# Two-layer hybrid encoder on one core: the start's transfers reordered, the final norm's last columns taken from PSUM, the output stored in three parts

## The chip, the cores and the metric

The kernel runs on 1 core of a Trainium2 chip. The metric is the device time of one execution in microseconds (us). Engines are named as in the profile: PE is TensorE, ACT ScalarE, DVE VectorE, POOL GpSimd, SP SyncE, which here only issues transfers.

## The reference, cut to what matters

256 tokens of 1024 channels pass through two layers. Each has a token mixer and a gated MLP, both behind an RMSNorm and with a residual, and a last RMSNorm makes the output. All is float32.

```python
def _rmsnorm(x, g):
    y = x * lax.rsqrt(jnp.mean(x * x, axis=-1, keepdims=True) + EPS)
    return y * g

h = x
for layer in range(DEPTH):                      # DEPTH = 2
    h = h + _token_mixer(_rmsnorm(h, norm1[layer]), w_in[layer], ...)
    h = h + _conv_ffn(_rmsnorm(h, norm2[layer]), w_up[layer], ..., w_down[layer])
return _rmsnorm(h, norm_f)
```

## The kernel before, in words

Tokens lie on the 128 partitions in two tiles, t = 0 and 1; `h` (128 x 2 x 1024) holds the residual stream in SBUF for the whole program. Each weight is streamed once from HBM by SP, in pieces named `raw`, and split into a rounded high part `wh` (ACT, L191 or L199) and a low part `wl` (DVE, L192 or L200). Products are float32r matmuls: high x high, low x high, high x low. The scheduler of the framework orders each engine's instructions; in the first stage (`values_of_x`, L702) the order is that of the code.

**The start.** `begin` (L337) issues the first transfers: pieces of the value weights `raw` (L142), pieces of x into `h` (L343), and the 8 x 128 row `grows` of norm1 (L349). PE meanwhile multiplies a tile of ones by itself (`warm`, L374, result unused), transposes the row so that the gains lie on partitions (L369; DVE copies it to `gcol`, L370), and transposes the first 256 columns of x for both tiles (`turn_x`, L715). One more warming matmul follows (`wait`, called at L790). ACT scales the first weights by `gcol` (L199) as it rounds them, so the first product (`product`, L762) needs the row, the first piece of x and the first piece of weights. The norm's factor of each token is applied to the finished sums.

**The end.** `residual_mm` (L567) adds `w_down`'s product to the residual: all but the last 4 of 22 chunks are added for both tiles and all columns into four PSUM banks `ps[t][c]` of 512 columns; the last 4 chunks (`held`) are then added one segment of columns after another (L593): for t = 0 two of 512, for t = 1 columns 0 to 511, 512 to 767 and 768 to 1023. The third segment of t = 1 shares its bank with the second; so DVE first adds the bank's partial sum to `h` (L599), and the last 4 chunks go to a tile of their own, `res2_ps` (L600; profile and order call it `res_ps`). After each segment `Norm.add` (L456) lets DVE add the sum to `h` (L460), ACT square the new columns and sum them up (L462, which in the profile is an ACTIVATE and the read of its accumulator), DVE multiply them by the final gain into `xn` (L467), and POOL add up the sums (L469, L471). After a tile's last segment POOL takes the power -1/2 (L474), and `store` (L509) scales `xn` by this factor `rstd`, columns 0 to 511 on DVE and the others on ACT, and sends both halves out on SP. The store of t = 0 is run within t = 1's segments.

## Time and profile before

| | us |
|---|---|
| median of 3 runs (860.9, 860.95, 861.31) | 860.95 |
| profiled execution, whole | 860.72 |
| its span, first to last instruction | 858.9 |
| PE busy | 850.1 |

A row of the timeline gives the start in us from the span's start, the duration, the engine, the line, the operation and its tiles, and in brackets the engine's idle time before it with what ended it. `SPq` and `ACTq` are the engines' queues issuing a transfer. PE's matmuls overlap, so the distance of two starts, not the duration, is what one of a row of them costs. A row of the chain gives start, duration and what the end of the program hung on at that time.

### The profile page before, as it was taken

Reading aid. Unit: us, or ns where it says so; the run is one execution under the profiler, and the core shown is the slowest. Engines: PE = TensorE matmul, PEld = TensorE weight load, DVE = VectorE, ACT = ScalarE, POOL = GpSimd, SP = SyncE. Lnnn points to the kernel's source line nnn. Section 1 sums busy time; section 2 is a strip of 40 time slices with the busy share of each in tenths; the row PEclk is TensorE's granted clock in tenths of the full one; section 3 lists DMA queues with packets and bytes.
Section 4 is the critical chain, followed back from the end, with each engine's and each line's share of the span. In section 5 each row is a group of like instructions: output and inputs, shape, how many; then the busy total and the mean of one; then the engine's idle time right before and its main releaser. Section 6 shows DMA issues by size and latency. Waiting matters only on the chain.

```text
span 858.9 us, 11272 instructions
## 1 busy us (share of the span) xinstructions
PE 850.1 (99%) x4036; PEld 714.3 (83%) x4036; DVE 646.1 (75%) x910; ACT 478.7 (56%) x702; POOL 19.0 (2%) x54
## 2 busy tenths in 40 slices
PE   8999999999999999999999999999999999999997
PEld 7888898888888888888888889888888888888885
DVE  4967989566757699999555598886567757998974
ACT  7735475444535576767344446654445436666762
POOL 1120000000010000000000000000000000000001
PEclk9999999999999999999999999999999999999999
DMA  9687585763846777877526776648558376777751
GB/s 316 201 280 248 173 286 157 221 234 123 295 171 212 238 241 242 249 238 270 196 98 201 231 235 206 223 156 247 199 201 285 103 214 211 242 242 240 240 197 50
DMA packets 99628, 185.02 MB, mean 215 GB/s; under 512 B 9630, under 2 KB 26734, under 8 KB 99572
## 3 DMA queue, kind: packets, MB, share of 16 engines
q1 hardware_dynamic: 98900, 182.83, 65.0%
q0 software_dynamic: 528, 1.34, 0.6%
q8 instruction: 32, 0.52, 0.2%
q14 instruction: 24, 0.20, 0.1%
q10 hardware_dynamic: 144, 0.13, 0.0%
HBM read 160.12 MB, written 1.07 MB: 188 GB/s over the span
## 4 chain that ended last, share of the span: by engine, by line
PE 99%; DMA 0%; ACT 0%; issue 0%; POOLq 0%; DVE 0%; POOL 0%; ACTq 0%
PE rows_ps L649 61%; PE res_ps L563 6%; PE res_ps L564 6%; PE res_ps L565 6%; PE v_ps L649 5%; PE proj_ps L535 3%; PE v_ps L765 3%; PE proj_ps L537 2%; PE s_ps L1053 1%; PE o_ps L1128 1%; PE s_ps L1048 1%; PE o_ps L1124 1%; PE xt_ps L496 1%; PE pool_ps L528 0%; PE pool_ps L527 0%; PE pool_ps L529 0%
## 5 line engine op out<-in xcount | busy, mean ns | idle before, releaser
L192 DVE TENSOR_TENSOR wl<-raw,wh 128x1024 fp32r<-128x1024 f32 x278 | 337.0, 1218 | 148.0 <-ACT wh L191 145.6
L649 PE MATMUL rows_ps<-wh,x 128*128 128x512 f32 x1344 | 420.1, 391 | 0.0
L191 ACT CAST wh<-raw 128x1024 fp32r<-128x1024 f32 x278 | 288.9, 1048 | 212.2 <-PE rows_ps L649 129.8
L649 PEld LDWEIGHTS rows_ps<-wh,x 128*128 128x128 f32 x1344 | 252.4, 188 | 52.1
L649 PE MATMUL rows_ps<-wl,x 128*128 128x512 f32 x672 | 261.7, 389 | 0.0
L649 PEld LDWEIGHTS rows_ps<-wl,x 128*128 128x128 f32 x672 | 126.3, 188 | 25.6
L563 PE MATMUL res_ps<-wh,actq 128*128 128x512 f32 (+1 forms) x152 | 57.5, 379 | 0.0
L565 PE MATMUL res_ps<-wh,actk 128*128 128x512 f32 (+1 forms) x152 | 57.5, 378 | 0.0
L564 PE MATMUL res_ps<-wl,actq 128*128 128x512 f32 (+1 forms) x152 | 57.5, 378 | 0.0
L649 PE MATMUL rows_ps<-wh,po 128*128 128x512 f32 x128 | 41.2, 393 | 0.0
L563 PEld LDWEIGHTS res_ps<-wh,actq 128*128 128x128 f32 x152 | 28.6, 188 | 5.4
L565 PEld LDWEIGHTS res_ps<-wh,actk 128*128 128x128 f32 x152 | 28.6, 188 | 5.3
L564 PEld LDWEIGHTS res_ps<-wl,actq 128*128 128x128 f32 x152 | 28.6, 188 | 5.3
L535 PE MATMUL proj_ps<-x,wh 128*128 128x512 f32 x128 | 32.2, 394 | 0.0
L684 DVE STREAM_TRANSPOSE up_rows<-rows_ps 128x512 f32<-128x512 f32 x40 | 26.3, 693 | 3.1 <-PE rows_ps L649 3.1
L649 PEld LDWEIGHTS rows_ps<-wh,po 128*128 128x128 f32 x128 | 24.1, 188 | 4.9
L462 ACT ACTIVATE junk<-h 128x512 f32<-128x512 f32 (+1 forms) x20 | 10.9, 547 | 30.8 <-DVE h L460 30.8
L1356 ACT ACTIVATE yg<-a,prm 128x256 f32<-128x256 f32 x44 | 26.5, 602 | 1.5
L563 PE MATMUL res_ps<-wh,m 128*128 128x512 f32 (+1 forms) x72 | 26.9, 374 | 0.0
L535 PEld LDWEIGHTS proj_ps<-x,wh 128*128 128x128 f32 x128 | 23.1, 189 | 4.2
L565 PE MATMUL res_ps<-wh,m 128*128 128x512 f32 (+1 forms) x72 | 26.4, 367 | 0.0
L564 PE MATMUL res_ps<-wl,m 128*128 128x512 f32 (+1 forms) x72 | 26.4, 366 | 0.0
(214 smaller groups left out, 1051.0 us busy)
## 6 DMA issues: line engine op xcount, KB each, us to landing
raw<-in_w_in_dram SPq DMA_DIRECT2D x56, 1024.0 KB, 5.3
raw<-in_w_up_dram SPq DMA_DIRECT2D x40, 1024.0 KB, 6.3
raw<-in_w_down_dram SPq DMA_DIRECT2D x22, 1024.0 KB, 5.1
up_turned<-up_rows SPq DMA_DIRECT2D x160, 64.0 KB, 3.9
raw<-in_w_a_dram SPq DMA_DIRECT2D x8, 1024.0 KB, 5.4
raw<-in_w_o_dram SPq DMA_DIRECT2D x8, 1024.0 KB, 6.9
qk<-qk_rows SPq DMA_DIRECT2D x64, 64.0 KB, 2.1
pt<-rows SPq DMA_DIRECT2D x64, 64.0 KB, 3.7
```

Source lines behind the costliest of these rows:

```text
L191: lambda: nc.scalar.copy(out=h, in_=src),
L192: lambda: nc.vector.tensor_sub(out=l, in0=src, in1=h.bitcast(F32)),
L462: nc.scalar.activation(junk[:, 0 : cc.stop - cc.start], h[:, t, cc], AF.Square, scale=D**-0.5, accum_out=ss[:, n : n + 1],)
L535: nc.tensor.matmul(ps, wh(k), x2[:, k], start=(k == 0), stop=False)
L537: nc.tensor.matmul(ps[:, 1], wl(k), x2[:, k, 0], start=False, stop=(k == nk - 1))
L563: nc.tensor.matmul(ps, ah, wh, start=first, stop=False)
L564: nc.tensor.matmul(ps, ah, wl, start=False, stop=False)
L565: nc.tensor.matmul(ps, al, wh, start=False, stop=last)
L649: nc.tensor.matmul(ps, x2[:, 2 * n + j, part, t, :], w[:, j, :], start=(n + m == 0), stop=(n == of - 1 and m == 5),)
L684: nc.vector.transpose(out=out[:, :, t].rearrange("p j c r -> p c j r"), in_=ps[t].rearrange("p (c j r) -> p c j r", c=4, j=4),)
L765: return nc.tensor.matmul(ps[g][t], a[:, k, t, :], w[:, k % 2, :], start=k == 0 and kind == "hh", stop=k == KD - 1 and kind == "hl",)
L1356: nc.scalar.activation(y, aj, AF.Identity, bias=b, scale=w1)
```

## The change

At the start, norm1's row goes out on ACT's queue instead of POOL's, as the first transfer there; all pieces of x and of the weights go out on SP, x's first piece ahead of the weights. The transposes of t = 1 come after the warming matmul instead of ahead of it.

At the end, for the last layer only (`seeded`), t = 1's segments are done in the order 512 to 767, 0 to 511, 768 to 1023. After the first of them DVE adds the partial sum of columns 768 to 1023 to `h` as before, and then this part of `h` is split into a high and a low part (`seed`, on ACT and DVE). In the last segment PE adds both to `res2_ps`, with an identity `one_r` as the other operand, behind the first two of the four chunks; so `res2_ps` ends as the new `h` itself (`whole`), and DVE's addition at the end is left out: ACT squares and DVE multiplies straight from PSUM. `store` sends columns 0 to 319 and 320 to 639 from DVE by SP and columns 640 to 1023 from ACT by ACT's own queue.

```diff
@@ -339,14 +339,14 @@
 
         loads = [W.load_by(n) for n in (4, 4, 2, 2)]
 
-        def part_of_x(t, c, queue=nc.sync):
-            queue.dma_start(out=h[:, t, c], in_=xv[:, t, c])
+        def part_of_x(t, c):
+            nc.sync.dma_start(out=h[:, t, c], in_=xv[:, t, c])
 
         first, second, others = slice(0, 256), slice(256, 512), slice(512, D)
+        rows8 = sm.tile([KD, P], F32, tag="gain", bufs=1, name="grows")
+        nc.scalar.dma_start(out=rows8, in_=norm1[0].rearrange("(k p) -> k p", p=P))
+        part_of_x(0, first)
         next(loads[0])
-        part_of_x(0, first, nc.scalar)
-        rows8 = sm.tile([KD, P], F32, tag="gain", bufs=1, name="grows")
-        nc.gpsimd.dma_start(out=rows8, in_=norm1[0].rearrange("(k p) -> k p", p=P))
         part_of_x(1, first)
         next(loads[1])
         next(loads[0])
@@ -453,18 +453,16 @@
             self.xn = big.tile([P, 2, D], F32, tag="xn", name="xn")
             self.ss = [sm.tile([P, 4], F32, tag="ss", name="ss") for _ in range(2)]
 
-        def add(self, t, n, cc, ps=None):
+        def add(self, t, n, cc, ps, whole=False):
 
             ss = self.ss[t]
-            if ps is not None:
+            junk = sm.tile([P, 512], F32, tag="s", name="junk")[:, 0 : cc.stop - cc.start]
+            if not whole:
                 nc.vector.tensor_add(out=h[:, t, cc], in0=ps, in1=h[:, t, cc])
-            junk = sm.tile([P, 512], F32, tag="s", name="junk")
-            nc.scalar.activation(
-                junk[:, 0 : cc.stop - cc.start], h[:, t, cc], AF.Square, scale=D**-0.5,
-                accum_out=ss[:, n : n + 1],
-            )
+            new = ps if whole else h[:, t, cc]
+            nc.scalar.activation(junk, new, AF.Square, scale=D**-0.5, accum_out=ss[:, n : n + 1])
             if self.ahead is not None:
-                nc.vector.tensor_mul(out=self.xn[:, t, cc], in0=h[:, t, cc], in1=self.ahead[:, cc])
+                nc.vector.tensor_mul(out=self.xn[:, t, cc], in0=new, in1=self.ahead[:, cc])
             if n == 0:
                 nc.gpsimd.tensor_scalar_add(ss[:, 3:4], ss[:, 0:1], EPS)
             else:
@@ -508,10 +506,12 @@
 
     def store(t, r, xn):
         ov = out[0].rearrange("(m t) d -> m t d", t=2)
-        nc.vector.tensor_scalar_mul(xn[:, 0:512], xn[:, 0:512], r[:, 0:1])
-        nc.sync.dma_start(out=ov[:, t, 0:512], in_=xn[:, 0:512])
-        nc.scalar.mul(out=xn[:, 512:], in_=xn[:, 512:], mul=r[:, 0:1])
-        nc.sync.dma_start(out=ov[:, t, 512:], in_=xn[:, 512:])
+        b = slice(640, D)
+        for c in (slice(0, 320), slice(320, 640)):
+            nc.vector.tensor_scalar_mul(xn[:, c], xn[:, c], r[:, 0:1])
+            nc.sync.dma_start(out=ov[:, t, c], in_=xn[:, c])
+        nc.scalar.mul(out=xn[:, b], in_=xn[:, b], mul=r[:, 0:1])
+        nc.scalar.dma_start(out=ov[:, t, b], in_=xn[:, b])
         yield
 
     later = []
@@ -564,7 +564,7 @@
         nc.tensor.matmul(ps, ah, wl, start=False, stop=False)
         nc.tensor.matmul(ps, al, wh, start=False, stop=last)
 
-    def residual_mm(parts, n, done, hold=4, fill=None, ahead=0):
+    def residual_mm(parts, n, done, hold=4, fill=None, ahead=0, seeded=False):
 
 
 
@@ -590,16 +590,27 @@
                 held.append((i, part))
             yield
         then, half = None, None
+        seed = None
+        if seeded:
+            one_r = sm.tile([P, P], F32R, tag="u", name="one_r")
+            nc.scalar.copy(out=one_r, in_=ident)
         for t in range(2):
-            for m, cc in enumerate(SEGMENTS[t]):
+            segments = SEGMENTS[t]
+            if t and seeded:
+                segments = segments[1], segments[0], segments[2]
+            for m, cc in enumerate(segments):
                 c, c0 = divmod(cc.start, 512)
                 res = ps[t][c][:, c0 : c0 + cc.stop - cc.start]
                 if c0:
 
-                    nc.vector.tensor_add(out=h[:, t, cc], in0=res, in1=h[:, t, cc])
+                    if not seed:
+                        nc.vector.tensor_add(out=h[:, t, cc], in0=res, in1=h[:, t, cc])
                     res = mmp.tile([P, cc.stop - cc.start], F32, tag="mm", name="res2_ps")
                 for j, (i, part) in enumerate(held):
                     one(part, res, t, cc, c0 != 0 and j == 0, j == hold - 1)
+                    if c0 and j == 1:
+                        for more in seed or ():
+                            nc.tensor.matmul(res, one_r, more, start=False, stop=False)
                 if half:
                     run(half)
                     half = None
@@ -607,7 +618,13 @@
                     half = then()
                     next(half)
                     then = None
-                then = done(t, m, cc, res) or then
+                then = done(t, m, cc, res, c0 != 0 and seeded) or then
+                if t and seeded and m == 0:
+                    rest = slice(768, D)
+                    hi, lo = seed = [sm.tile([P, 256], F32R, tag="us", name="seed") for _ in range(2)]
+                    nc.vector.tensor_add(out=h[:, t, rest], in0=ps[t][1][:, 256:], in1=h[:, t, rest])
+                    nc.scalar.copy(out=hi, in_=h[:, t, rest])
+                    nc.vector.tensor_sub(out=lo, in0=h[:, t, rest], in1=hi.bitcast(F32))
         if half:
             run(half)
         rest = fill() if fill else None
@@ -786,8 +803,9 @@
             return lambda: nc.vector.tensor_sub(out=ol, in0=f, in1=oh.bitcast(F32))
 
         fs = [big.tile([P, 4, 2, P], F32, tag=tag, name="xu") for tag in ("q0", "k0")]
-        (keep0, copy0), (keep1, copy1) = turn_x(0, 0, 2), turn_x(1, 0, 2)
+        keep0, copy0 = turn_x(0, 0, 2)
         wait()
+        keep1, copy1 = turn_x(1, 0, 2)
         rest = keep0(nc.vector.tensor_copy)
         low = split(0, 0)
         rest()
@@ -1408,7 +1426,7 @@
 
         down = residual_mm(
             lambda k: acts[k], NF, lambda *a: late["norm"].add(*a),
-            fill=begin_values if l + 1 < DEPTH else None, ahead=3,
+            fill=begin_values if l + 1 < DEPTH else None, ahead=3, seeded=l + 1 == DEPTH,
         )
         count, twos, open_two = 0, [], []
```

What it moves on the engines' queues, at three places. First SP at the program's start (`raw` with a number is a piece of weights, `h` a piece of x), before:

```order
L142 DMA raw_88<-in_w_in_dram 128x512
L343 DMA h<-in_x_dram 128x256
L142 DMA raw_94<-in_w_in_dram 128x512
L142 DMA raw_88<-in_w_in_dram 128x512
L343 DMA h<-in_x_dram 128x256 x2
```

and now:

```order
L343 DMA h<-in_x_dram 128x256
L142 DMA raw_91<-in_w_in_dram 128x512
L343 DMA h<-in_x_dram 128x256
L142 DMA raw_94<-in_w_in_dram 128x512
L142 DMA raw_91<-in_w_in_dram 128x512
```

One transfer of x, which was on ACT's queue, heads SP's; every later transfer of SP stands one place further back.

Second, PE up to the first product (`gain_ps` is the transposed row, `xt_ps` the transposed x, `v_ps` the product; in brackets the semaphores waited for, DMAHW being transfers of SP and ACT, DMASW those of POOL), before:

```order
L377 MATMUL gain_ps<-ones 128x128 x4
L369 MATMUL gain_ps<-ident,grows 128x8 [waits DMASW0_49,Pool_49]
L719 MATMUL xt_ps<-ident,h 128x128 [waits DMAHW0_49]
L719 MATMUL xt_ps<-ident,h 128x128 [waits DMAHW2_49]
L377 MATMUL warm_ps<-ones 128x128
L765 MATMUL v_ps<-m_151,xuh 128x512 [waits DVE_49,Activation_49]
```

and now:

```order
L377 MATMUL gain_ps<-ones 128x128 x4
L369 MATMUL gain_ps<-ident,grows 128x8 [waits DMAHW0_49,Pool_49]
L736 MATMUL xt_ps<-ident,h 128x128 [waits DMAHW1_49]
L377 MATMUL warm_ps<-ones 128x128
L736 MATMUL xt_ps<-ident,h 128x128 [waits DMAHW3_49]
L782 MATMUL v_ps<-m_151,xuh 128x512 [waits DVE_49,Activation_49]
```

The warming matmul has moved ahead of the transposes that wait for x's second piece (each of these rows of `xt_ps` is followed by one more without a wait, left out here).

Third, ACT's last instructions, from the last split of weights on (`junk` is the square's unused result, `ss` its sum), before:

```order
L191 CAST wh_7379<-raw_7325 128x1024
L462 ACTIVATE junk,ss<-h 128x512 x2
L513 ACTIVATE xn<-xn,rstd 128x512
L462 ACTIVATE junk,ss<-h 128x512
L462 ACTIVATE junk,ss<-h 128x256 x2
```

and now:

```order
L191 CAST wh_7379<-raw_7325 128x1024
L463 ACTIVATE junk,ss<-h 128x512 x2
L513 ACTIVATE xn<-xn,rstd 128x384
L463 ACTIVATE junk,ss<-h 128x256
L626 CAST seed<-h 128x256
L514 DMA out_dram<-xn 128x384
L463 ACTIVATE junk,ss<-h 128x512
L463 ACTIVATE junk,ss<-res_ps 128x256
```

The seed's cast and the issue of t = 0's store stand between the squares, and the last square reads `res_ps` in PSUM; in both, t = 1's scaling by `rstd` follows. On DVE, t = 0's store now stands ahead of the seed's low part, this ahead of the addition of columns 0 to 511, and the last multiplication by the gain waits for ACT.

## The prediction

> **What bounds the kernel now.** I read the page first, for the share of each engine and for the chain that ended last.
>
> ```profile
> PE 850.1 (99%) x4036; PEld 714.3 (83%) x4036; DVE 646.1 (75%) x910; ACT 478.7 (56%) x702; POOL 19.0 (2%) x54
> PEclk9999999999999999999999999999999999999999
> PE 99%; DMA 0%; ACT 0%; issue 0%; POOLq 0%; DVE 0%; POOL 0%; ACTq 0%
> ```
>
> TensorE works 850.1 of 858.9 us and is 99% of the chain. The 8.8 us in which it is idle can only lie at the ends, so an edit is worth what it does to the first matmuls, to what follows the last one, and to TensorE's own work. The second view is the chain of the first 26 us.
>
> ```profile
> 1.27 3.60 DMA grows<-in_norm_dram
> ...
> 5.25 1.04 PE xt_ps L719 x4
> 6.30 0.43 PE warm_ps L377 x2
> 6.72 4.53 PE v_ps L765 x12
> ```
>
> The first 5 us belong to one 4 KB transfer, norm1's row, issued by POOL at 1.27 and landed 3.60 us later. Behind it stand four transposes (1.04), the warming matmul (0.43), and then the products of the values without a gap. The third view is the timeline of TensorE there.
>
> ```profile
> 1.04 2.50 PE L377 MATMUL gain_ps<-ones 128*128 128x128 f32 x10 [1.04 <-DVE mhalf L366]
> 5.01 0.24 PE L369 MATMUL gain_ps<-ident,grows 8*128 8x8 f32 x1 [1.46 <-DMA grows<-in_norm_dram]
> 6.48 0.76 PE L765 MATMUL v_ps<-m,xuh 128*128 128x512 f32 x1
> 9.60 0.63 PE L765 MATMUL v_ps<-wh,xul 128*128 128x512 f32 x1
> 10.03 0.53 PE L765 MATMUL v_ps<-wl,xuh 128*128 128x512 f32 x1
> 10.40 0.39 PE L765 MATMUL v_ps<-wh,xuh 128*128 128x512 f32 x1
> 10.63 0.39 PE L765 MATMUL v_ps<-wh,xul 128*128 128x512 f32 x1
> ```
>
> Two things are to be seen. TensorE warms from 1.04 to 3.54, waits 1.46 us for the row, and starts the first product at 6.48. And equal matmuls follow each other by 0.43 us (9.60 to 10.03) until about 10.3 and by 0.23 us (10.40 to 10.63) from then on. The page's row of the granted clock reads 9 in all slices and doesn't show this step; the starts do. TensorE runs at 0.23/0.43 = 0.53 of its speed until 10.3. The burst of 2.50 us did not end the slow stretch; it ended 5.3 us after work was taken up at 5.01.
>
> **The start.** The transfers are reordered, and one of two pairs of transposes now stands behind the warming matmul. These are the rows that price it.
>
> ```profile
> 0.72 0.41 ACTq L343 DMA_DIRECT2D h<-in_x_dram  x1
> 0.73 0.39 SPq L142 DMA_DIRECT2D raw<-in_w_in_dram  x1
> 1.17 0.42 SPq L343 DMA_DIRECT2D h<-in_x_dram  x1
> 1.64 0.91 SPq L142 DMA_DIRECT2D raw<-in_w_in_dram  x2
> ...
> raw<-in_w_in_dram SPq DMA_DIRECT2D x6, 256.0 KB, 3.7
> ...
> 5.49 0.72 ACT L199 ACTIVATE m<-raw,gcol 128x512 fp32r<-128x512 f32 x1 [2.84 <-DVE gcol L370]
> 6.33 0.37 ACT L726 CAST xuh<-xt_ps 128x256 fp32r<-128x256 f32 x1
> ...
> 11.51 0.37 ACT L726 CAST xuh<-xt_ps 128x256 fp32r<-128x256 f32 x1 [1.09 <-PE xt_ps L719]
> ```
>
> *The row.* It takes the ACT slot at 0.72. This trace has no small transfer on that queue at the start: at the short end the output's 2.0 us (row below), at the long end the weights' 3.7 us. So it lands between 2.7 and 4.4; I take 3.3, nearer the short end because it is 4 KB. TensorE is busy warming until 3.54 anyway, so the transposed row comes at 3.75, and t=0's two transposes (half of 1.04 for four) and the warming matmul (0.43) run until 4.7.
>
> *What is late next.* The first weights move from SP's slot at 0.73 to the one at 1.17; with 3.7 us they land at 4.87. ScalarE's high part takes 0.72, so it is done at 5.65. The second piece of x moves from 1.17 to 1.64; it lands by 5.36 at the worst, by 4.6 if its half size halves the time beyond the first 2 us; I take 4.9, and its two transposes end at about 5.4. The first product needs both and starts at about 5.6 (5.3 to 6.0 between the ends), instead of at 6.48. TensorE's pauses between 3.54 and 5.6 are then some 0.6 us instead of 1.46.
>
> *What that is worth.* The 0.88 us are won in the slow stretch. If the speed still rises at 10.3, TensorE has done 0.88 x 0.53 = 0.47 us of full-speed work more by then, and the start gives **0.47 us** (0.25 to 0.65 for the two ends). Later loads shift by one slot of 0.45 us; ScalarE, which splits them, waits for TensorE 1.09 us at 11.51, so this is covered. POOL loses the issue and makes the identity earlier, which nobody waits for.
>
> [...]
>
> **The end.** The timeline from t=1's first matmul on:
>
> ```profile
> 846.87 0.39 PE L563 MATMUL res_ps<-wh,actq 128*128 128x512 f32 x1
> 849.59 0.72 ACT L513 ACTIVATE xn<-xn,rstd 128x512 f32<-128x512 f32 x1 [1.02 <-POOL rstd L474]
> 851.84 0.42 ACT L462 ACTIVATE junk<-h 128x256 f32<-128x256 f32 x1 [0.34 <-DVE h L460]
> 852.22 0.28 PE L564 MATMUL res_ps<-wl,actq 128*128 128x256 f32 x1
> 852.34 0.28 PE L565 MATMUL res_ps<-wh,actk 128*128 128x256 f32 x1
> 852.66 0.42 DVE L460 TENSOR_TENSOR h<-res_ps,h 128x256 f32<-128x256 f32 x1 [0.25 <-PE res_ps L565]
> 853.17 0.42 ACT L462 ACTIVATE junk<-h 128x256 f32<-128x256 f32 x1 [0.83 <-DVE h L460]
> 853.50 0.19 ACT L462 ACTIVATION_READ_ACCUMULATOR junk<-h 128x1 f32 x1
> 853.83 0.19 POOL L471 TENSOR_TENSOR ss<-ss 128x1 f32<-128x1 f32 x1 [1.14 <-ACT junk L462]
> 854.10 0.57 POOL L474 TENSOR_TENSOR rstd<-ss,mhalf 128x1 f32<-128x1 f32 x1
> 854.70 0.72 ACT L513 ACTIVATE xn<-xn,rstd 128x512 f32<-128x512 f32 x1 [1.01 <-POOL rstd L474]
> 854.70 0.49 DVE L511 TENSOR_SCALAR xn<-xn,rstd 128x512 f32<-128x512 f32 x1 [1.16 <-POOL rstd L474]
> 855.21 0.33 SPq L512 DMA_DIRECT2D out_dram<-xn  x1
> 855.60 0.42 SPq L514 DMA_DIRECT2D out_dram<-xn  x1
> ...
> out_dram<-xn SPq DMA_DIRECT2D x4, 256.0 KB, 2.0
> ```
>
> *Removed:* VectorE's addition at 852.66 from the chain. TensorE ends at 852.62, the square begins at 853.17: 0.55 us. ScalarE now waits for TensorE itself; VectorE's own wait took 0.04 us, so the square begins 0.05 us after TensorE. That saves 0.50. Reading 256 columns from PSUM took ScalarE 0.37 (the cast at 6.33) against 0.42 for the square: no loss.
>
> *Added on TensorE:* two seed matmuls of 256 columns, 0.12 us each by the two starts at 852.22 and 852.34: 0.24. Net 0.26 from TensorE's end to the norm's factor.
>
> *The seed's own path.* TensorE asks for it after t=1's 12 matmuls of 256 columns, 12 of 512 and 6 more of 256: 846.87 + 12 x 0.12 + 12 x 0.23 + 6 x 0.12 = 851.8. On ScalarE its cast stands behind t=0's store, which waits for its factor until 849.59: 384 columns by share of 0.72, some 0.6; then a square (0.42 and its read, 0.5 together) and the cast, 0.4: 851.1. VectorE's low part adds 0.45: 851.55. It is in time by 0.2 us; each 0.1 us beyond that is 0.1 at the end. Behind it on VectorE stands the addition of columns 0 to 511, which would have been ready at 851.2 and now starts at 851.55; its square then ends just before the last one may start at 852.9. This is the tightest cover of the edit. The cast of the identity stands on ScalarE near 830, where
>
> ```profile
> 836.23 1.05 ACT L191 CAST wh<-raw 128x1024 fp32r<-128x1024 f32 x1 [1.66 <-PE res_ps L565]
> ```
>
> shows ScalarE waiting 1.66 us for TensorE: nothing.
>
> *Store.* VectorE's first piece falls from 512 to 320 columns: between 0.31 (by share of 0.49) and 0.49; I take 0.36. So the first issue goes out 0.26 + 0.13 earlier than 855.21. ScalarE's piece of 384 columns ends some 0.6 after the factor and is issued on its own queue; the last issue then starts near 855.2 instead of 855.60. The bytes are the same and each transfer took 2.0 us; three transfers instead of two could cost up to 0.3 us again. I take **0.35 us** for the end (0 to 0.5).
>
> VectorE's multiplication of the PSUM columns by the gain waits for ScalarE's square, as the order shows, and behind it stands the store's first piece. It begins when the square's value is read, at 853.45, and takes 0.42, while POOL needs its 0.19, 0.57 and the gaps until 854.4: covered by 0.5 us. [...]
>
> **Sum.** The profiled execution took 860.72 us, 1.8 more than its span; the median of the runs is 860.95, 0.23 above it. 860.72 - 0.47 - 0.35 = 859.9; against the median 860.1.
>
> **The rivals.**
>
> *The speed rises earlier.* For it: the pause of 1.46 us becomes some 0.6 in pieces, so the burst at 1.04 and the rest may count as one. If work from 1.04 on is counted as that from 5.01 was, the rise comes 5.3 us after it, at 6.4. Before, the slow products from 6.48 to 10.33 were worth 3.85 x 0.53 = 2.04 us of full speed; now 5.6 to 6.4 is worth 0.42, and the remaining 1.62 is done at 8.0: 2.3 us won instead of 0.47. ScalarE then has to keep up; its slack of 1.09 us at 11.51 may cost some 0.3. With the end this gives 860.95 - 2.0 - 0.35 = 858.6, or 858.2 without a loss. Against it: a burst of 2.50 us was not enough, pauses remain, and transposes fill part of the time.
>
> *The row isn't the only thing that was late.* If the weights, one slot later, or the second piece of x land at 5.5 or later, the first product stays near 6.48 and only the end is left: 860.6. For it: in the trace the transfers crowd between 1 and 5 us. Against it: 3.7 us from 1.17 is 4.87.
>
> *Slower.* A pause in the slow stretch starts the count anew. After 5.6 the first place where this could happen is the third chunk of weights: if TensorE pauses for it near 8.5, the rise comes 5.3 us after it, near 13.8. Each us by which the rise slips past 10.3 costs 0.47; it decides from a slip of 0.82/0.47 = 1.7 us. At 13.8 it costs 1.6: 861.8. Against it: at 0.43 us each, the twelve products before that place keep TensorE until 10.7, and ScalarE has the chunk split by 8.2 in the trace.
>
> **How the numbers follow.** The forecast has a chance of 0.52, the earlier rise 0.36, a start without gain 0.08, the later rise 0.04. About 0.2% (1.7 us) is what a measurement of this kernel can tell from no change. The forecast, 859.7 to 860.7 on its own, is within that, as are the start without gain and the later rise; the earlier rise is faster. With a fast edge of the forecast and a late seed on top of a later rise I give 0.40 faster, 0.57 same, 0.03 slower. The range is 858.1 to 860.9: it takes in the earlier rise and the start without gain.
>
> **What would show it.** In the changed profile: the first product's start (5.6 forecast; 6.4 or later refutes the start), the place where equal matmuls go from 0.43 to 0.23 apart (10.3, or 6.4 to 7), and the pauses of TensorE between 3.5 and 6. At the end: the square 0.05 us after TensorE's last matmul, no pause ahead of the seed's two matmuls, the first output issued 2.2 us after TensorE's end instead of 2.6. A pause ahead of the seed, or a last square that waits for the one before it, would make the end wrong; a rise at another time makes the start wrong.

## The result and the profile after

The changed kernel took 858.70 us (median of 13 executions, 858.17 to 859.44); the kernel before took 860.54 (13 executions, 859.85 to 861.31). The ratio is 0.9978 with a 95% interval of 0.997 to 0.9985: 1.84 us or 0.2% faster. That is inside the range of the prediction and near the time of its second case, the earlier rise of the speed (858.6), not at the likeliest value of 860.1. The profiled execution of the changed kernel took 859.44 us with a span of 857.7; it is the slowest of the 13, so the two profiles differ by 1.28 us only. Two executions in a slow state are left out of everything below, one of 972.35 us in the last group of experiments and one of the kernel before of 3059.01 us.

The page of the changed kernel, its first row of busy time and the chain that ended last:

```profile
PE 850.5 (99%) x4038; PEld 713.2 (83%) x4038; DVE 646.5 (75%) x912; ACT 477.6 (56%) x704; POOL 18.4 (2%) x53
PE 88%; DVE 5%; DMA 4%; SPq 1%; ACT 1%; issue 1%; POOLq 0%; DVEq 0%; POOL 0%; ACTq 0%
```

TensorE has the two seed matmuls more (4038 for 4036) and is still 99% of the span. But the chain is no longer TensorE alone: 12% of it are something else, above all VectorE and transfers. That is not time lost: most of it lies between 700 and 808 us, behind one wait of TensorE of 0.30 us, which is shown below. Where the program is pulled forward, something else sets the pace for a while. The timeline of the start shows the first such place.

```profile
0.72 0.59 ACTq L347 DMA_DIRECT2D grows<-in_norm_dram  x1
3.48 0.27 PE L369 MATMUL gain_ps<-ident,grows 8*128 8x8 f32 x1
3.68 0.69 PE L736 MATMUL xt_ps<-ident,h 128*128 128x128 f32 x2
4.20 0.72 ACT L199 ACTIVATE m<-raw,gcol 128x512 fp32r<-128x512 f32 x1 [1.36 <-DMA raw<-in_w_in_dram]
4.66 0.69 PE L736 MATMUL xt_ps<-ident,h 128*128 128x128 f32 x2
5.00 0.77 PE L782 MATMUL v_ps<-m,xuh 128*128 128x512 f32 x1
6.00 1.13 PE L782 MATMUL v_ps<-m,xuh 128*128 128x512 f32 x3
6.96 0.39 PE L782 MATMUL v_ps<-m,xul 128*128 128x512 f32 x1
7.20 0.40 PE L782 MATMUL v_ps<-wh,xuh 128*128 128x512 f32 x1
7.43 0.39 PE L782 MATMUL v_ps<-wh,xul 128*128 128x512 f32 x1
7.88 0.72 ACT L199 ACTIVATE m<-raw,gcol 128x512 fp32r<-128x512 f32 x1 [1.06 <-DMA raw<-in_w_in_dram]
9.22 0.72 ACT L199 ACTIVATE wh<-raw,gcol 128x512 fp32r<-128x512 f32 x1 [0.36 <-DMA raw<-in_w_in_dram]
9.44 0.30 PEld L782 LDWEIGHTS v_ps<-m,xuh 128*128 128x128 f32 x2 [0.45 <-DVE m L200]
```

Three things are to be seen. The row is there when the warming matmuls end: its transpose starts at 3.48 with no wait of TensorE, where the kernel before waited 1.46 us. The first product starts at 5.00 for 6.48. And equal matmuls are 0.23 us apart from 6.96 on (6.96, 7.20, 7.43), which before began after 10.03: the trace's record of the granted clock begins at 6.61 here and at 10.33 before. (Ahead of that first entry the views print a granted clock of 1.00, so they don't show the slow stretch; the distance of equal matmuls does.) Then the gain starts to go: at 7.88 and 9.22 ScalarE starts late on the third and fourth pieces of weights, for which it has waited 1.06 and 0.36 us, and at 9.44 TensorE's weight load has waited 0.45 us for the part made of the third piece.

How much goes is read from the same instructions in the two traces, the pairs and the eight transposes of x, before:

```profile
11.09 0.38 PE L719 MATMUL xt_ps<-ident,h 128*128 128x128 f32 x2
12.69 0.38 PE L719 MATMUL xt_ps<-ident,h 128*128 128x128 f32 x2
17.02 1.03 PE L719 MATMUL xt_ps<-ident,h 128*128 128x128 f32 x8
```

and after:

```profile
8.58 0.38 PE L736 MATMUL xt_ps<-ident,h 128*128 128x128 f32 x2
10.50 0.38 PE L736 MATMUL xt_ps<-ident,h 128*128 128x128 f32 x2
15.57 1.03 PE L736 MATMUL xt_ps<-ident,h 128*128 128x128 f32 x8
```

The lead is 1.48 us at the first product, 2.51 at the first pair, 2.19 at the second, 1.45 at the eight. So 1.06 us are given back between 8.6 and 15.6. Two more waits of TensorE's weight load lie in that stretch, 0.54 us at 12.38 and 0.49 at 13.16, for weights that ScalarE and VectorE have to split. The chain of these microseconds shows what stands behind them:

```profile
5.43 4.42 DMA h<-in_x_dram
9.85 1.32 ACT junk L754 x4
11.70 0.63 ACT m L199
12.36 0.76 DVE m L200
13.16 2.57 PE v_ps L782 x10
```

A piece of x that was issued at 5.43 has landed by 9.85, just as ScalarE is through with the fourth piece of weights; two squares of x (1.32) and two copies follow on ScalarE, and only then the next weights. So it isn't late weights alone that take the lead back: ScalarE, once late, has no pause in which to catch up. No run here parts the two.

In this execution another 0.5 is lost on the way to 808, in the MLP of the last layer, where TensorE has a wait that the kernel before doesn't have (the same matmul started at 809.01 there, so the lead is 0.95):

```profile
808.06 0.50 PE L564 MATMUL res_ps<-wl,actq 128*128 128x512 f32 x1 [0.30 <-DVE wl L192]
```

The end of the changed kernel, in its timeline:

```profile
850.12 0.43 DVE L627 TENSOR_TENSOR seed<-h,seed 128x256 fp32r<-128x256 f32 x1 [0.66 <-ACT seed L626]
850.94 0.40 PE L613 MATMUL res_ps<-seed,one_r 128*128 128x256 f32 x2
852.14 0.38 ACT L463 ACTIVATE junk<-res_ps 128x256 f32<-128x256 f32 x1 [0.24 <-PE res_ps L565]
852.65 0.42 DVE L465 TENSOR_TENSOR xn<-res_ps,gain 128x256 f32<-128x256 f32 x1 [0.77 <-ACT junk L463]
853.03 0.57 POOL L472 TENSOR_TENSOR rstd<-ss,mhalf 128x1 f32<-128x1 f32 x1
853.63 0.61 ACT L513 ACTIVATE xn<-xn,rstd 128x384 f32<-128x384 f32 x1 [1.01 <-POOL rstd L472]
853.63 0.68 DVE L511 TENSOR_SCALAR xn<-xn,rstd 128x320 f32<-128x320 f32 x2 [0.56 <-POOL rstd L472]
```

TensorE ends at 852.05. The square follows 0.09 us later, and the scaling by the factor starts 1.58 us after TensorE's end; before it was 2.08 (852.62 to 854.70). The addition's 0.50 us are gone from the chain, as predicted. From TensorE's end to the end of the span it is 5.62 us for 6.32 (spans of 857.66 and 858.94), 0.70 less; minus the two seed matmuls (0.24) this leaves 0.46.

### The profile page after: what moved, and what is told of

Its sections match the earlier page's. It is cut to its first block, busy times and chain, and to the rows that moved or that the text cites. A ratio compares the mean times of both kernels' runs of the same rounds, so it can differ in the third digit from the quotient of the medians.

```text
span 857.7 us, 11279 instructions
## 1 busy us (share of the span) xinstructions
PE 850.5 (99%) x4038; PEld 713.2 (83%) x4038; DVE 646.5 (75%) x912; ACT 477.6 (56%) x704; POOL 18.4 (2%) x53
## 4 chain that ended last, share of the span: by engine, by line
PE 88%; DVE 5%; DMA 4%; SPq 1%; ACT 1%; issue 1%; POOLq 0%; DVEq 0%; POOL 0%; ACTq 0%
PE rows_ps L666 53%; PE res_ps L564 6%; PE res_ps L565 6%; PE res_ps L563 6%; PE v_ps L666 5%; PE proj_ps L535 3%; DMA raw<-in_w_up_dram 2%; DVE wl L192 2%; PE v_ps L782 2%; PE proj_ps L537 2%; PE s_ps L1071 1%; PE o_ps L1146 1%; SPq L691 1%; DMA raw<-in_w_down_dram 1%; PE s_ps L1066 1%; PE o_ps L1142 1%
```

## The experiments

Two theories stand against each other for the start. **The clock:** the matmul rate steps from 0.43 to 0.23 us at the end of the first stretch of some 3.4 us that TensorE fills (in the changed kernel it is busy for all of the 3.41 us up to the step at 6.61, in the kernel before for 1.95 of the 3.41 us up to 6.91); the pause before the row's transpose kept such a stretch from being filled, and closing it is worth more than the earlier product. **The path:** only the earlier first product counts. The experiments ran in three groups, each in turn with the kernel before: the first four here (its median 860.53), then the whole end and the addition alone on the quiet base, the transposes and x's first piece (860.46), then the rest (860.56). So a difference of 0.1 us between kernels of different groups, or between one of them and the changed kernel (860.54), tells nothing. The interval of each ratio is some 0.7 us to either side; what is said of smaller differences rests on medians of 11 executions.

### The change's start alone

The kernel before with `begin()` and the order of the transposes of the changed kernel:

```diff
-        part_of_x(0, first, nc.scalar)
-        nc.gpsimd.dma_start(out=rows8, in_=norm1[0].rearrange("(k p) -> k p", p=P))
+        nc.scalar.dma_start(out=rows8, in_=norm1[0].rearrange("(k p) -> k p", p=P))
+        part_of_x(0, first)
...
-        (keep0, copy0), (keep1, copy1) = turn_x(0, 0, 2), turn_x(1, 0, 2)
+        keep0, copy0 = turn_x(0, 0, 2)
         wait()
+        keep1, copy1 = turn_x(1, 0, 2)
```

> The change's start (row on ScalarE's queue, x and weights on SyncE's, x's second transpose behind the warming pair) with the old end. Theory A, the clock: most of the gain at the start comes from the rate of the matmuls, which steps from 0.43 to 0.23 us at the end of the first stretch of some 3.4 us that TensorE fills; with the pause of 1.46 us gone the step comes between 4.5 and 7.9 us instead of at 10.3, and part of what that brings is given back to late transfers: 1.0 to 1.8 us faster than the kernel before, 1.4 the likeliest. Rival B, the path: only the earlier first product counts (5.0 for 6.5 us), the step stays near 10: 0.3 to 0.7 us faster, and the rest of the change's 1.84 us would have to lie at the end.

859.13 us, ratio 0.9985 (0.9976 to 0.9993): 1.40 faster.

```profile
5.18 0.50 PE L765 MATMUL v_ps<-m,xuh 128*128 128x512 f32 x1
```

The first product starts at 5.18, and the record of the granted clock begins at 5.21. The clock's number, 1.4, is met; the path's 0.3 to 0.7 isn't. That leaves 0.43 us for the end (859.13 less 858.70).

### The change's end alone

The changed kernel with the same lines turned back: the old start, the new `Norm.add`, `store` and `residual_mm`.

> The change's end (addition put into PSUM by two matmuls, output in three parts) with the old start. Theory A: the path of the two profiles gives 0.39 us (factor 0.50 earlier, first issue another 0.09, landings 0.04, less 0.24 for the two matmuls): 0.2 to 0.55 us faster than before, step of the matmul rate where the kernel before has it, 8.4 to 11.8 us. Rival B: the end carries the larger part, 1.1 to 1.5 us faster.

860.59 us, ratio 0.9999 (0.999 to 1.0008): no gain by the median, 0.23 by the mean (860.27 for 860.50). It doesn't decide, and its spread says why: 859.15 to 860.91. The execution that was profiled is the one of 859.15, and there the rate steps early although the start is the old one:

```profile
7.31 1.17 PE L782 MATMUL v_ps<-m,xuh 128*128 128x512 f32 x3
8.32 0.39 PE L782 MATMUL v_ps<-m,xul 128*128 128x512 f32 x1
8.55 0.39 PE L782 MATMUL v_ps<-wh,xuh 128*128 128x512 f32 x1
8.78 0.39 PE L782 MATMUL v_ps<-wh,xul 128*128 128x512 f32 x1
```

The spacing is 0.23 from 8.32 on; the clock's record begins at 7.99, in the profile of before at 10.33. With the same start the full rate came at different times in these two executions, and the spread of the times covers the end's 0.4.

### Nothing but more warming

```diff
-WARM = (5, 1)
+WARM = (8, 1)
```

in the kernel before: eight warming matmuls ahead of the row's transpose. No transfer and no order changes.

> The kernel before with eight warming matmuls ahead of the row instead of five, so that the pause of 1.46 us ahead of the row's transpose is filled with products that nobody reads; no transfer and no order is changed. Theory A, the clock: the step of the rate from 0.43 to 0.23 us comes between 4.5 and 7.9 us though the first product stays at 6.5 us or comes up to 0.2 later: 0.8 to 1.7 us faster than before. Rival B, the path: nothing that anyone waits for comes earlier: no gain, 0 to 0.2 us slower.

859.25 us, ratio 0.9988 (0.9979 to 0.9996): 1.28 faster, and the spread shrinks to 0.51 us (858.99 to 859.50). Its timeline:

```profile
1.04 3.78 PE L377 MATMUL gain_ps<-ones 128*128 128x128 f32 x16 [1.04 <-DVE mhalf L366]
4.92 0.24 PE L369 MATMUL gain_ps<-ident,grows 8*128 8x8 f32 x1
6.39 0.47 PE L765 MATMUL v_ps<-m,xuh 128*128 128x512 f32 x1
7.99 0.39 PE L765 MATMUL v_ps<-m,xul 128*128 128x512 f32 x1
8.21 0.40 PE L765 MATMUL v_ps<-wh,xuh 128*128 128x512 f32 x1
15.52 1.03 PE L719 MATMUL xt_ps<-ident,h 128*128 128x128 f32 x8
```

The row comes as late as before (4.92), and so does the first product (6.39 for 6.48), but the pause is filled and the full rate is granted from 6.15. The eight transposes of x are reached at 15.52, 1.50 us earlier than before and 0.05 earlier than in the changed kernel. Three products that nobody reads bring, in the kernel before, nine tenths of what the change's start brings. The path's expectation, no gain, falls.

### The changed kernel without the five warming matmuls

```diff
-WARM = (5, 1)
+WARM = (0, 1)
```

> The changed kernel without the five warming matmuls ahead of the row: TensorE starts near 3.5 us instead of 1.04, and the first product stays at 5.0 us. Theory A, the clock: the stretch that has to be filled starts 2.4 us later, so the step comes between 6.9 and 10.3 us; it loses 0.5 to 1.2 us to the changed kernel, so 0.6 to 1.3 us faster than before. Rival B, the path: the first product is where the changed kernel has it, so the time is too: 1.6 to 2.0 us faster than before.

858.86 us, ratio 0.9981 (0.9972 to 0.999): 0.16 slower than the changed kernel. The path's number is met: 1.67 faster than before, for 1.6 to 2.0. The clock's expectation fails: it put the loss at 0.5 to 1.2 and the rise at 6.9 to 10.3.

```profile
3.26 0.69 PE L736 MATMUL xt_ps<-ident,h 128*128 128x128 f32 x2 [0.77 <-DMA h<-in_x_dram]
```

In the profile TensorE starts at 2.25 and works from 3.26 on almost without a pause, and the full rate is granted from 6.54, as early as in the profile of the changed kernel (6.61). So in the changed kernel the warming matmuls are worth nothing that these times can tell, and this run doesn't speak for the clock. An execution in which it falls later loses less than the slow products cost, since the lead is given back to transfers before 15 us anyway; this last step is argued, not shown.

### The parts of the end, on the quiet base

Since eight warming matmuls leave little spread, the end was taken apart there: the whole new end, the addition through PSUM with the output in two parts, and the output in three parts alone.

> The kernel before with eight warming matmuls (whose executions lie within 0.5 us of each other, where those of before spread over 1.5) and the whole new end. Theory A, the path of the profiles: the end is worth 0.39 us, so 0.25 to 0.5 us faster than eight warming matmuls alone (which took 859.25), about 858.9, 1.5 to 1.75 faster than before. Rival, from the median of the end alone (860.59, no gain): the end is worth nothing, 859.2 to 859.3.

> Eight warming matmuls and the new end without the output in three parts: addition through PSUM, output in two parts on SyncE's queue as before. Theory A: factor 0.50 us earlier, less 0.24 for the two matmuls: 0.15 to 0.35 us faster than eight warming matmuls alone, 858.9 to 859.1. Rival: the three parts carry the gain of the end and the addition none, 859.2 to 859.3.

> The kernel before with eight warming matmuls and only the output in three parts; addition and square as before. Theory Z: as eight warming matmuls alone, 859.15 to 859.35. Rival P, the prediction: 0.1 to 0.15 us faster, 859.05 to 859.15. If the two parts of the end add up, what it saves and what the addition through PSUM saves (0.46 by the medians) come to what the whole end saved there (0.34).

And the changed kernel with the old `store`, which is also what the addition alone has:

```diff
-        b = slice(640, D)
-        for c in (slice(0, 320), slice(320, 640)):
-            nc.vector.tensor_scalar_mul(xn[:, c], xn[:, c], r[:, 0:1])
-            nc.sync.dma_start(out=ov[:, t, c], in_=xn[:, c])
-        nc.scalar.mul(out=xn[:, b], in_=xn[:, b], mul=r[:, 0:1])
-        nc.scalar.dma_start(out=ov[:, t, b], in_=xn[:, b])
+        nc.vector.tensor_scalar_mul(xn[:, 0:512], xn[:, 0:512], r[:, 0:1])
+        nc.sync.dma_start(out=ov[:, t, 0:512], in_=xn[:, 0:512])
+        nc.scalar.mul(out=xn[:, 512:], in_=xn[:, 512:], mul=r[:, 0:1])
+        nc.sync.dma_start(out=ov[:, t, 512:], in_=xn[:, 512:])
```

> The changed kernel with the output in two parts on SyncE's queue. Theory Z: 858.5 to 858.85, as the changed kernel. Rival P, the prediction: 0.1 to 0.15 us slower than the changed kernel, 858.8 to 859.0.

| kernel | us | ratio to before (95%) |
|---|---|---|
| eight warming matmuls | 859.25 | 0.9988 (0.9979 to 0.9996) |
| with the whole new end | 858.91 | 0.9982 (0.9973 to 0.9991) |
| with the addition through PSUM alone | 858.79 | 0.9981 (0.9972 to 0.999) |
| with three output parts alone | 859.22 | 0.9984 (0.9975 to 0.9992) |
| changed kernel | 858.70 | 0.9978 (0.997 to 0.9985) |
| changed kernel, two output parts | 858.71 | 0.9981 (0.9972 to 0.9989) |

The end is worth 0.34 us here (0.27 if each is taken from the kernel before of its own group) and 0.43 by the start alone: the prediction's 0.35. By the medians all of it is the addition through PSUM, which comes to 0.46 alone, 0.31 with three parts and 0.42 behind the new start. The three parts come to -0.03, +0.12 and -0.01 (minus is faster) by the three pairs of medians: nothing. In the profiles they do shorten the stretch behind TensorE's end, by 0.13 or 0.14 in each pair: 6.19 us for 6.32 with the old addition, 5.69 for 5.82 with the new one, 5.62 for 5.76 in the changed kernel. That this 0.13 doesn't show in the times stays open: the medians can't tell 0.1 with certainty, and no run shows anything that the three parts make slower.

From the start of the factor's computation to the first issue it is 1.02 us with three parts (852.27 to 853.29, the whole end on the quiet base) and 1.12 with two (852.15 to 853.27, the addition alone); to the last issue 1.44 (853.71) and 1.50 (853.65). So the last transfer starts hardly earlier, and it is smaller.

### x's second transpose back ahead of the warming pair

```diff
-        keep0, copy0 = turn_x(0, 0, 2)
+        (keep0, copy0), (keep1, copy1) = turn_x(0, 0, 2), turn_x(1, 0, 2)
         wait()
-        keep1, copy1 = turn_x(1, 0, 2)
```

in the changed kernel.

> The changed kernel with x's second transpose ahead of the warming pair, as before the change: TensorE waits for x's second piece (4.61 us) with nothing beside it, a pause of some 0.5 us instead of 0.15, and the pair stands between it and the first product, which comes at 5.5 to 5.7 us instead of 5.0. Theory T: the weights' transfers set the time at 8 to 13 us anyway, so this is taken up: 0 to 0.25 us slower than the changed kernel. Rival C: the pause leaves a clock window unfilled, or the product's delay counts whole: 0.4 to 1.0 us slower, 859.1 to 859.7.

858.61 us, ratio 0.9982 (0.9973 to 0.9991): as the changed kernel by the median, though two of the eleven executions took 859.66 and 860.48. The first product came at 5.21, not at 5.5 or later, since x's second piece had landed at 4.40. The order of the transposes, one of the change's three edits at the start, is worth nothing that this median shows.

### One piece of x back on ScalarE's queue, behind the row

The lead that is given back between 8 and 15 us goes first to pieces of weights, which stand one place later on SyncE's queue than before. Two kernels take one place out again, the first with x's first piece, the second with x's piece of the other row block:

```diff
-        part_of_x(0, first)
+        part_of_x(0, first, nc.scalar)
```

> The changed kernel with x's first piece on ScalarE's queue behind the row, so that SyncE issues every later transfer one place (0.47 us) earlier. Theory Q, the queue: the third and fourth pieces of weights, which landed at 7.86 and near 9.2 us, land 0.4 to 0.7 us earlier, TensorE's waits for them at 9 to 13 us shrink, though x's first piece comes up to 0.6 us later: 0.3 to 0.6 us faster than the changed kernel, 858.1 to 858.4. Rival R, the rate: the transfers move no faster and the third piece lands where it did: within 0.2 us of the changed kernel, 858.5 to 858.9, or slower if x's first piece delays the first product by more than the transfers take back.

859.01 us, ratio 0.9983 (0.9974 to 0.9992): 0.3 slower than the changed kernel. The third and fourth pieces did what theory Q says: they landed at 7.46 and 8.80, 0.40 us earlier each, ScalarE took them up at 7.72 and 8.82, and TensorE has no wait at 9 to 13 us. The second piece came later, at 6.82 for 5.82, which held ScalarE up for 0.64 us. But x's first piece now came later:

```profile
4.25 0.69 PE L736 MATMUL xt_ps<-ident,h 128*128 128x128 f32 x2 [0.50 <-DMA h<-in_x_dram]
5.55 0.76 PE L782 MATMUL v_ps<-m,xuh 128*128 128x512 f32 x1
```

TensorE pauses 0.50 us ahead of x's transposes, the first product starts at 5.55, and the clock's record begins at 8.34. These are the two stretches of 3.41 us ahead of that; the first column of work is TensorE's.

```profile
1.52:4.93 3.41, 2.91 (x14) 2.59 (x14) 0.17 (x1) 2.20 (x3) 0.00 (x0) 1.00 0.83 231
4.93:8.34 3.41, 3.41 (x12) 2.70 (x11) 2.59 (x5) 1.87 (x4) 0.00 (x0) 1.00 0.91 305
```

TensorE was busy for 2.91 of the 3.41 us up to 4.93, with no step of the rate there, and for all of the 3.41 us up to the step at 8.34. In the profile of the changed kernel, without this pause of half a microsecond, the step came at 6.61.

```diff
-        part_of_x(1, first)
+        part_of_x(1, first, nc.scalar)
```

> The changed kernel with the second row block's first piece of x, not the first one's, behind the row on ScalarE's queue: the piece that the first product needs stays first on SyncE's queue, and SyncE issues every later transfer one place (0.47 us) earlier. Theory G, transfers take back 0.8 to 1.1 us at 8 to 15 us: the third piece of weights lands near 7.4 us instead of 7.86, the first product stays near 5.0, and TensorE's waits shrink by about as much: 0.2 to 0.5 us faster than the changed kernel, 858.2 to 858.5. Rival: the waits are made by ScalarE's order of work and not by the landing, or another wait takes their place: 858.6 to 858.9.

859.27 us, ratio 0.9984 (0.9976 to 0.9993), spread 857.79 to 860.20. Theory G's number isn't met by the median. The chain of its first 10 us shows what took the place of the wait:

```profile
1.34 4.08 DMA h<-in_x_dram
5.46 0.69 PE xt_ps L736 x2
6.15 3.87 PE v_ps L782 x9
```

The piece on ScalarE's queue needed 4.08 us (the trace lands it at 5.42; in the changed kernel, issued at 1.64, it landed at 4.61), and the first weights beside it landed at 5.24 for 4.11. TensorE paused 0.67 us ahead of the transposes, was busy for 2.74 of the 3.41 us from 2.71 to 6.12, and the rate rose at 9.53. Its best execution, 857.79, is 0.38 faster than the best of the changed kernel; without a trace of that execution nothing shows when its rate rose.

The same with the output in two parts:

> The same with the output in two parts on SyncE's queue as before the change. Theory Z, the three parts are worth nothing: within 0.15 us of x's second piece behind the row alone. Rival P, the prediction: an earlier first issue and smaller last part were worth 0.1 to 0.15 us, so it is that much slower.

859.39 us, ratio 0.9981 (0.9972 to 0.999): within 0.15 of the three parts, as theory Z says, but with the same wide spread, so it proves little. In its profile TensorE was busy for 3.02 of the 3.41 us from 3.59 to 7.00, and the rate rose at 10.41 only.

```profile
3.59:7.00 3.41, 3.02 (x10) 2.15 (x11) 2.17 (x6) 1.82 (x4) 0.00 (x0) 1.00 1.03 372
7.00:10.41 3.41, 3.41 (x10) 2.64 (x9) 2.19 (x3) 2.89 (x8) 0.43 (x2) 1.00 0.97 325
```

No kernel beats the changed one's median by more than its measurement is uncertain.

## Why the prediction was right or wrong

**The bound.** That everything lies at the two ends holds for where the time came from. It isn't the whole account: 1.06 us of the start's lead went between 8.6 and 15.6 us, and in the profiled execution another 0.5 by 808.

**The row.** Right in effect: it was there when the warming ended, and the transposed row came at 3.75 as predicted (3.48 and 0.27). It had landed earlier than the shortest estimate, 2.7: without warming its transpose starts at 2.25.

**What is late next.** The mechanism was right and the sizes too large. The weights landed at 4.11, not 4.87 (2.9 us after their issue, not 3.7), x's second piece at 4.61, not 4.9; so the first product came at 5.00, not 5.6, below even the short end of 5.3.

**What that is worth.** Here is the step that failed: "If the speed still rises at 10.3 ... the start gives **0.47 us**", taken as the likeliest with 0.52. The speed rose at 6.61, and the start gave 1.40 us. The case with the earlier rise, at 0.36, had the direction right; its cause, a burst and the rest counting as one, is borne out by the eight warming matmuls, which fill the pause and change nothing else: a rise at 6.15, and 1.28 us. That its time of 858.6 is 0.1 from the measured one is in part luck: it took 2.0 us for the start where the runs show 1.40, and it took them from 860.95, the median of three executions, where 13 gave 860.54. Its place, 6.4, is near the 6.61 of one execution; with the same start the rise came at 5.21 (the start alone) and 7.12 (the changed kernel with two output parts). What stood against it in the prediction, "a burst of 2.50 us was not enough, pauses remain, and transposes fill part of the time", was weighed wrongly. By the table in the last section, the 3.41 us up to 3.50 began 0.95 us ahead of TensorE's first matmul (0.72 busy) and the next 3.41 us had the pause of 1.46 us in them (0.57); that this, and not a burst that was spent, is why the rate didn't rise there is the author's reading. Behind it stood a wrong idea of the row of 5.3 us "after work was taken up": with the same start and work taken up at 4.85 the rise came 3.1 us later (the end alone, 7.99). The rows of one execution showed one sample of a moment that differs between executions.

**The later loads.** "Later loads shift by one slot of 0.45 us; ScalarE ... waits for TensorE 1.09 us at 11.51, so this is covered." Wrong: once TensorE is 2.5 us ahead the slack is used up. ScalarE took up the third piece at 7.88 after a wait of 1.06 us, was without slack from then on, and 1.06 us of TensorE's lead was given back (nothing shown here makes the two figures equal). With eight warming matmuls, whose lead of 1.50 us isn't given back, the eight transposes come as early as in the changed kernel: what the earlier first product adds to the earlier rise (859.25 with the old end against 859.13 with the new start) is 0.12 us by the medians. The rival's loss for this, "some 0.3", was a third of it.

**The end.** Right in sum and in most terms: factor 0.50 earlier, seeds 0.24, 0.46 in the profile and 0.27 to 0.43 by the runs, for 0.35 predicted. The seed was ready at 850.55 and asked for at 850.94: 0.4 us to spare, twice the 0.2 predicted, and TensorE doesn't pause there. The last multiplication by the gain waited for the square (0.77 us, 852.65) and ended at 853.07, 0.56 ahead of the store. The store's 0.13 is there in the profiles, in all three pairs; the times show none of it, and they show 0.31 to 0.46 for the addition, for which the working gives 0.26. So the sum is borne out by the runs, its split isn't.

**The slower case.** The rise didn't slip behind 10.3 in the changed kernel. In the kernel with x's second piece behind the row it came late, at 9.53, behind a pause of 0.67 us, and at 10.41 with two output parts; but that pause lies ahead of the first product and not at the third chunk. That a pause starts a count of 5.3 us anew isn't borne out: work was taken up at 5.46 there, 4.07 us ahead of the rise, and at 4.85 in the end alone, 3.14 us ahead of it.

## What to carry to other kernels

Ahead of the first real matmul, try to fill the pauses of TensorE with products that nobody reads, up to the moment when the data come: in the kernel before that alone gave 1.28 us, where the whole change gives 1.84, and in one execution with a pause of 0.5 us the rate rose at 8.34, for 6.61 in the changed kernel. It isn't always worth something: in the changed kernel the five warming matmuls could be left out for 0.16 us. Find out from several executions where the matmul rate steps before pricing a start by it, and price an earlier start only up to the next transfer or engine that was just in time: of the lead of 2.51 us here, 1.06 were given back by 15.6. To measure an edit of some tenths of a microsecond, first make a base that spreads little.

## What the runs showed of the hardware

**The moment of full rate.** In the kernel before the granted clock's record runs from 10.327 to 856.832 us, in the changed one from 6.605 to 856.524: 846.505 and 849.919 us, 3.414 apart. In the twelve profiles of the table it begins between 4.33 and 10.41 us. Counted back from there in stretches of 3.41 us, TensorE was busy for these shares of them (ahead of 1.04 it does no work):

| profile | earlier stretches | stretch up to the rise | rise, us |
|---|---|---|---|
| before | 0.72, 0.57 | 1.00 | 10.33 |
| changed | 0.63 | 1.00 | 6.61 |
| start alone | 0.22 | 1.00 | 5.21 |
| end alone | 0.70 | 0.92 | 7.99 |
| eight warming matmuls | 0.50 | 0.97 | 6.15 |
| changed, no warming | 0.07 | 0.92 | 6.54 |
| eight, whole end | 0.21 | 0.95 | 5.17 |
| eight, three parts alone | 0.00 | 0.96 | 4.33 |
| changed, two parts | 0.78 | 1.00 | 7.12 |
| x's first piece behind the row | 0.14, 0.85 | 1.00 | 8.34 |
| x's second piece behind the row | 0.49, 0.80 | 1.00 | 9.53 |
| the same, two parts | 0.74, 0.89 | 1.00 | 10.41 |

In these twelve executions the stretches up to the rise were busy to between 0.92 and 1.00, the earlier ones to between 0.00 and 0.89; that shows no rule. Unread products and transposes are among the work. In the three parts alone on the quiet base the stretch up to the rise, 0.92 to 4.33, holds nothing but warming matmuls (3.29 us). In the changed kernel, by the starts of its timeline, 1.02 us of the 3.41 from 3.19 to 6.60 are transposes (3.48 to 4.16 and 4.66 to 5.00); without them it would be 0.70, less than the 0.72 of warming products alone in the kernel before, behind which the rate didn't rise. In the end alone 1.08 us of the stretch up to the rise are transposes; without them it would be 0.60. Two of the stretches as the trace has them, one without a rise in the kernel before and the one up to the rise in the end alone (first column of work: TensorE):

```profile
3.50:6.91 3.41, 1.95 (x9) 1.78 (x9) 1.14 (x4) 1.30 (x3) 0.00 (x0) 1.00 1.09 369
...
4.57:7.98 3.41, 3.13 (x11) 2.78 (x12) 2.36 (x6) 2.23 (x5) 0.00 (x0) 1.00 0.96 302
```

How much of the spread of the times comes from this isn't shown, since each kernel has a trace of one execution only. With the same start the rise came at 10.33 in the kernel before and at 7.99 in the end alone: 2.34 us, which at 1 - 0.23/0.43 = 0.47 per us is 1.1 us, an estimate from the two spacings. The two executions took 860.72 and 859.15, 1.57 apart, of which the end is 0.34 to 0.43. The kernel before spread over 1.46 in 13 executions and over 1.48 to 1.88 in the three groups. With eight warming matmuls the rise came at 6.15, ahead of the first product at 6.39, and the times spread over 0.51. One execution of 860.49 with the whole new end on that base falls out of this.

**Early transfers.** In the five profiles in which all of x and the weights go over SyncE's queue, the transfers from 2 to 8 us ran at 248 to 269 GB/s; in the nine in which one early piece of x goes over ScalarE's queue, at 275 to 325. These are before and the changed kernel from 5 to 6 us, where the changed one moved least between 3 and 8; the last number is GB/s:

```profile
5.00:6.00 1.00, 0.99 (x5) 0.97 (x6) 0.26 (x2) 0.51 (x1) 0.00 (x0) 1.00 1.01 348
```

```profile
5.00:6.00 1.00, 1.00 (x5) 0.74 (x3) 1.00 (x3) 0.53 (x2) 0.00 (x0) 1.00 0.71 193
```

From 2 to 8 us the kernel before moved 312 GB/s and the changed one 263, so some 0.3 MB less by 8 us, a good piece of weights (256 KB). The fourteen traces show the two together, no more: the kernel with x's first piece behind the row is at 275, hardly above the five, and whether the second queue is the cause was not tried.

**A small transfer at the start.** The row's 4 KB on ScalarE's queue, issued at 0.72 in the changed kernel's trace, had landed by 2.25 us in that of the changed kernel without warming, when its transpose starts; the same row from GpSimd's queue, issued at 1.27, took 3.60 us.
